# Expert stages of a two-layer hybrid block on one core: instructions kept in the order of the source, and the one-hot matrix of the slot table built three weight units earlier

## The chip, the core and the metric

The kernel runs on one core of a Trainium2 chip. The metric is the device time of one execution in microseconds (us). The core's engines are named as the profile names them: PE (TensorE matmuls; PEld its weight loads), DVE (VectorE), ACT (ScalarE), POOL (GpSimd) and SP (SyncE, which here only issues transfers). Each engine works through its own list of instructions in order, and an instruction that waits holds up all that stand behind it on that engine.

## The reference

Two layers of a block with four mixers, then an expert-choice feed-forward net. The change touches only the last part, which in short is:

```python
def expert_choice_ffn(h, w_router, w_gate, w_up, w_down):
    n, dm = h.shape[1], h.shape[2]
    cap = EC_FACTOR * n // N_EXPERTS
    aff = jax.nn.softmax(jnp.einsum('bnd,de->bne', h, w_router).astype(jnp.float32), axis=-1)
    g, idx = lax.top_k(aff.swapaxes(1, 2), cap)
    xs = jax.vmap(lambda hb, ib: hb[ib])(h, idx)
    act = jax.nn.silu(jnp.einsum('becd,edf->becf', xs, w_gate)) * jnp.einsum('becd,edf->becf', xs, w_up)
    ys = jnp.einsum('becf,efd->becd', act, w_down) * g[..., None].astype(h.dtype)
    ...
```

There are 16 experts, a model width of 1024 and an expert width of 512. Each expert takes 128 of the 1024 tokens; in layer 0 it also takes 32 of the 256 context tokens with the same weights. Layer 1 needs no context.

## The kernel before

Mixers and expert stage of a layer are Python generators which a planner interleaves; when the expert stage runs, it is alone. What the generators emit is not yet the order on the chip: the framework's scheduler puts the instructions of every engine in an order of its own, from its own costs, unless a stretch is traced under `manual_schedule`, where the order of the source stays.

The expert stage is the function `experts`. Its weights come in 12 units of 512 KB for each expert: four units `k` = 0 to 3 (gate, up, gate, up), four of down, and `k` = 4 to 7. A round, the body of `for e in range(17)`, does for expert `e`: `gate_up` for `k` = 0 to 3; after `k` = 1 `turn(e - 1)`, which transposes the activations of the expert before; after `k` = 3 `prep(e + 2)`; in layer 0 `ctx`, the context's matmuls on the raw weights of the four units; `down(e - 1)`; `parts`, which transposes the gathered tokens of expert `e + 1`; `gate_up` for `k` = 4 to 7; `ctx` again; and `activate`.

`prep` makes the slot table: `onehot` compares each token's place with the slot number in eight DVE instructions (TENSOR_SCALAR, tile `M<-rc,pos`), eight small PE matmuls (`ps<-M,M`, 128x5) turn them into token numbers and gates, and POOL gathers the 128 tokens (`W<-dr,it`).

A weight unit passes four stations. SP loads it into one of 10 raw buffers (tile `C`). `issue` then splits it: ACT writes the high part (`A<-C`), DVE or, for two units of a round, POOL the low part (`A<-C,A`). The PE uses both. `gate_up` and `down` each call `issue` once, for the unit that stands 5 (layer 0) or 8 (layer 1) places further on. A raw buffer is free again in layer 0 when the context's matmuls on it are done, and in layer 1 when it is split; only then can SP load the unit that is 10 places further on:

```python
ahead, ring, raws = (5, 7, 10) if need else (8, 10, 10)
```

Of the kernel before, what the change touches and what calls it, by code (L numbers as in the profile page):

```python
# [163 lines left out]
class Model:  # L164
# [1573 lines left out]
                                    op0=ALU.is_equal)  # L1738
        return O

    def slots(self, e):

        nc = self.nc
        O = self.onehot(0, e, 8)
        po = self.p()
        for j in range(8):
            nc.tensor.matmul(po[:, 0:5], O[:, j], self.R[0][:, j, e, :], start=j == 0, stop=j == 7)
        sc = self.t("s1", [128, 5])
        nc.vector.tensor_copy(sc, po[:, 0:5])
        it = self.t("it", [128, 1], U32, bufs=4)  # L1750
        vt = self.t("vt", [128, 1], bufs=4)
        nc.vector.scalar_tensor_tensor(it, sc[:, 1:2], 128.0, sc[:, 0:1], op0=ALU.mult, op1=ALU.add)
        nc.vector.tensor_reduce(vt, sc[:, 2:5], axis=AX.X, op=ALU.add)
        return it, vt
# [32 lines left out]
    def experts(self, l, need, base, basec, h2d, h2c):  # L1787
# [5 lines left out]
        ahead, ring, raws = (5, 7, 10) if need else (8, 10, 10)  # L1793
# [30 lines left out]
        def issue(early=False):  # L1824
            nonlocal unit
            if not raw:
                return
            w = raw.pop(0)
            u = unit % ring
            hi, lo = rows[u], rows[ring + u]  # L1830
            nc.scalar.activation(hi, w, AF.Copy)
            (nc.gpsimd if early or unit % 6 == 5 else nc.vector).tensor_sub(lo, w, hi.bitcast(F32))
            unit += 1
            ready.append((w, hi, lo))
            if not need:
                fetch(1)

        def prep(e):
            it, vt = self.slots(e)
            X[e] = (self.gather(h2d, it), it, vt)  # L1840

        def gather_ctx(g):
# [15 lines left out]
        def parts(x):  # L1858

            x = x.rearrange("p (u n k) -> p u k n", u=4, k=2)  # L1860
            xh = self.t("W", [128, 8, 128], F32R)
            xl = self.t("W", [128, 8, 128], F32R)
            for hf in range(2):
                pt = self.p([128, 4, 128])
                for i in range(4):
                    nc.tensor.transpose(pt[:, i, :], x[:, 2 * hf + i // 2, i % 2], self.ident)
                hs = slice(4 * hf, 4 * hf + 4)
                nc.scalar.activation(xh[:, hs], pt, AF.Copy)
                nc.vector.tensor_sub(xl[:, hs], pt, xh[:, hs].bitcast(F32))
            return xh, xl  # L1870

        def gate_up(e, u, g, p):

            xh, xl = XT[e]
            w, hi, lo = ready.pop(0)
            for k in range(2):
                c = slice(512 * k, 512 * k + 512)
                for pas, (xx, ww) in enumerate(((xh, hi), (xl, hi), (xh, lo))):
                    nc.tensor.matmul(p, xx[:, 2 * u + k], ww[:, c], start=(u == 0 and k == 0 and pas == 0),
                                     stop=(u == 3 and k == 1 and pas == 2))  # L1880
            issue()
            return u, g, w

        def ctx(e, units, pc):

            cs = slice(32 * (e % 4), 32 * (e % 4) + 32)
            for u, g, w in units:
                for k in range(2):
                    for q in range(4):
                        nc.tensor.matmul(pc[32 * q:32 * q + 32, 128 * g:128 * g + 128], XC[e // 4][:, 2 * u + k, cs],  # L1890
                                         w[:, 512 * k + 128 * q:512 * k + 128 * q + 128], start=(u == 0 and k == 0 and g == 0),
                                         stop=(u == 3 and k == 1 and g == 1))
                fetch(1)
# [12 lines left out]
        def turn(e):  # L1906

            act, actc = ACT.pop(e)
            pt = self.p([128, 4, 128])
            for i in range(4):  # L1910
                nc.tensor.transpose(pt[:, i, :], act[:, 128 * i:128 * i + 128], self.ident)
            ah = self.t("M", [128, 4, 128], F32R)
            al = self.t("M", [128, 4, 128], F32R)
            nc.scalar.activation(ah, pt, AF.Copy)
            nc.vector.tensor_sub(al, pt, ah.bitcast(F32))
            ct = None
            if need:
                pt = self.p([128, 4, 128])
                nc.tensor.transpose(pt[:, 0, :], actc, self.ident)
                ct = self.t("M", [128, 128])  # L1920
                nc.scalar.activation(ct, pt[:, 0, :], AF.Copy)
            AT[e] = (ah, al, ct)

        def down(e):
            _, it, vt = X.pop(e)
            ah, al, ct = AT.pop(e)
            py = [self.p() for _ in range(2)]
            units = []
            for f in range(4):
                w, hi, lo = ready.pop(0)  # L1930
                for pas, (xx, ww) in enumerate(((ah, hi), (al, hi), (ah, lo))):
                    for hf in range(2):
                        nc.tensor.matmul(py[hf], xx[:, f], ww[:, 512 * hf:512 * hf + 512],
                                         start=(f == 0 and pas == 0), stop=(f == 3 and pas == 2))
                issue()
                units.append(w)
                yield "s"
            if need:
                pyc = self.p()
                for f, w in enumerate(units):  # L1940
                    for q in range(4):
                        nc.tensor.matmul(pyc[32 * q:32 * q + 32, :256], ct[:, 32 * f:32 * f + 32],
                                         w[:, 256 * q:256 * q + 256], start=f == 0, stop=f == 3)
                    fetch(1)
            ys = self.t("W", [128, D])
            for hf in range(2):
                c = slice(512 * hf, 512 * hf + 512)
                nc.vector.scalar_tensor_tensor(ys[:, c], py[hf], vt, G5[hf], op0=ALU.mult, op1=ALU.mult)
            nc.gpsimd.indirect_dma_start(out=base, out_offset=bass.IndirectOffsetOnAxis(ap=it, axis=0),
                                         in_=ys, in_offset=None, compute_op=ALU.add)  # L1950
            if need:
                yc = self.t("M", [128, 256])
                nc.vector.scalar_tensor_tensor(yc, pyc[:, :256], self.vc[:, e:e + 1], G5c, op0=ALU.mult, op1=ALU.mult)
                nc.gpsimd.indirect_dma_start(out=basec.rearrange("n (q d) -> (n q) d", q=4),
                                             out_offset=bass.IndirectOffsetOnAxis(ap=self.ic4[:, e:e + 1], axis=0),
                                             in_=yc, in_offset=None, compute_op=ALU.add)
# [17 lines left out]
            yield 3.0  # L1974
            turn_ctx(0)
        yield from self.wait(f"route{l}.0")
        prep(0)
        yield True
        prep(1)
        issue()  # L1980
        yield 3.0
        XT[0] = parts(X[0][0])
        while len(ready) < ahead:
            issue()
        for e in range(17):
            if e < 16:
                pg, pu = self.p(), self.p()
                pc = self.p() if need else None
                units = []
                for k in range(4):  # L1990
                    units.append(gate_up(e, k // 2, k % 2, (pg, pu)[k % 2]))
                    if k == 1 and e:
                        turn(e - 1)
                    if k == 3 and e + 2 < 16:
                        prep(e + 2)
                    yield "s"
                if need:
                    ctx(e, units, pc)
                    yield "s"
            else:  # L2000
                turn(e - 1)
            if e:
                yield from down(e - 1)
                yield "s"
            if e < 16:
                if e + 1 < 16:
                    if need and (e + 1) % 4 == 0:
                        turn_ctx((e + 1) // 4)
                    XT[e + 1] = parts(X[e + 1][0])
                    if need and e % 4 == 1 and e < 12:  # L2010
                        gather_ctx(e // 4 + 1)
                units = []
                for k in range(4, 8):
                    units.append(gate_up(e, k // 2, k % 2, (pg, pu)[k % 2]))
                    yield "s"
                if need:
                    ctx(e, units, pc)
                activate(e, pg, pu, pc)
            yield "s"

    def layer(self, l):
        need = l == 0
# [82 lines left out]
```

## Time and profile before

| what | value |
|---|---|
| median of 3 runs | 2949.53 us (2943.96 to 2954.22) |
| the profiled execution, and its span | 2941.95 us, 2940.1 us |
| PE busy over the span | 2499.6 us, 85% |
| DVE busy over the span | 1930.1 us, 66% |
| ACT, POOL busy | 1186.9 us (40%), 916.7 us (31%) |
| mean granted TensorE clock | 0.906 |

The expert stages are a small part of the program's instructions, but two stretches of the span: about 1130 to 1655 us (layer 0) and about 2580 to 2940 us (layer 1). A granted clock of 1.00 is 2.4 GHz and one of 0.50 is 1.2 GHz; a mean between them is a share of time at each. Nearly all instructions are recorded in the line of one helper (L160), so the rows are told apart by their tiles. The time outside the span in the profiled execution is 1.85 us.

### The profile page before, as it was taken

How to read it: one execution, taken by the hardware profiler on the slowest of the kernel's cores; microseconds unless marked ns; L12 is line 12 of the kernel's file. 1: busy time of each engine (PE TensorE's matmuls, PEld its weight loads, DVE VectorE, ACT ScalarE, POOL GpSimd, SP SyncE). 2: the span in 40 equal slices, each digit the busy share in tenths (PEclk: the TensorE clock that was granted, in tenths of full speed). 3: DMA queues.
4: the chain of work that ended last, by engine and by line, in shares of the span. 5: the costliest groups of instructions: out<-in, count | busy, mean ns of one | idle time of the engine just before them, and what ended most of it. 6: DMA issues, size and time to landing. Idle time of an engine off the chain costs nothing. (4 is left out here: it accounts for less than half of the span.)

```text
span 2940.1 us, 50544 instructions
## 1 busy us (share of the span) xinstructions
PE 2499.6 (85%) x19427; PEld 1879.6 (64%) x19427; DVE 1930.1 (66%) x3894; ACT 1186.9 (40%) x2010; POOL 916.7 (31%) x930
## 2 busy tenths in 40 slices
PE   6879989989997875888889699879878988579997
PEld 3658877545554654666656488779655556467776
DVE  5444575567775546666666656681778765679996
ACT  3354223244352122444445444342353342356664
POOL 3212332234421131233233432421353411324443
PEclk8889999999998887988889799989979999789998
DMA  6222235485214343666667711132331024569996
GB/s 241 61 65 63 75 107 162 154 276 200 65 63 142 111 168 116 226 237 224 229 205 263 229 47 37 51 97 77 115 111 53 22 93 138 213 225 338 347 342 207
DMA packets 243440, 455.45 MB, mean 155 GB/s; under 512 B 25688, under 2 KB 155096, under 8 KB 242176
## 3 DMA queue, kind: packets, MB, share of 16 engines
q1 hardware_dynamic: 190176, 365.75, 36.2%
q0 software_dynamic: 12096, 37.75, 5.7%
q10 hardware_dynamic: 40928, 48.72, 4.7%
q8 instruction: 153, 2.51, 0.4%
q14 instruction: 87, 0.71, 0.1%
HBM read 377.55 MB, written 74.60 MB: 154 GB/s over the span
## 5 line engine op out<-in xcount | busy, mean ns | idle before, releaser
L160 PE MATMUL ps<-A,W 128*128 128x512 f32 (+3 forms) x4160 | 968.9, 378 | 67.8 <-ACT W L160 31.5
L160 PEld LDWEIGHTS ps<-A,W 128*128 128x128 f32 x4160 | 735.9, 194 | 221.1 <-ACT W L160 35.4
L160 DVE TENSOR_TENSOR A<-C,A 128x1024 fp32r<-128x1024 f32 x310 | 458.0, 1496 | 155.3 <-ACT A L160 149.7
L160 ACT ACTIVATE A<-C 128x1024 fp32r<-128x1024 f32 x384 | 399.6, 1058 | 325.5 <-DMA C<-in_moe_w_gate_dram 119.7
L160 ACT ACTIVATE M<-ps 128x512 f32<-128x512 f32 (+6 forms) x576 | 264.2, 468 | 486.9 <-PE ps L160 404.5
L160 POOL TENSOR_TENSOR A<-C,A 128x1024 fp32r<-128x1024 f32 x74 | 200.9, 2719 | 214.0 <-ACT A L160 213.7
L160 PE MATMUL ps<-A,M 128*128 128x512 f32 x768 | 204.7, 420 | 1.1 <-ACT M L160 0.7
L160 PE MATMUL ps<-W,A 128*128 128x256 f32 x1344 | 191.7, 299 | 9.8 <-DVE A L160 8.8
L160 PEld LDWEIGHTS ps<-W,A 128*128 128x128 f32 x1344 | 176.5, 202 | 12.3 <-DVE A L160 9.3
L160 PE MATMUL ps<-C,A 128*32 128x128 f32 (+1 forms) x2528 | 183.0, 331 | 0.0
L160 PEld LDWEIGHTS ps<-A,M 128*128 128x128 f32 x768 | 151.8, 202 | 36.6 <-issue 5.2
L160 PE MATMUL ps<-M,M 128*128 128x64 f32 (+3 forms) x968 | 126.0, 254 | 54.6 <-DVE M L160 44.0
L160 POOL TENSOR_TENSOR C<-C,M 128x512 f32<-128x512 f32 x76 | 111.8, 1483 | 193.0 <-ACT M L160 132.8
L160 PE MATMUL ps<-cf,M 128*128 128x128 f32 (+3 forms) x416 | 75.3, 304 | 101.1 <-DVE M L160 67.9
L160 DVE TENSOR_TENSOR C<-C,M 128x512 f32<-128x512 f32 (+2 forms) x196 | 129.4, 672 | 40.7 <-ACT M L160 39.3
L160 PEld LDWEIGHTS ps<-C,A 128*32 128x32 f32 (+1 forms) x2528 | 143.6, 140 | 9.4 <-issue 5.3
L160 PE MATMUL ps<-A 96*128 96x512 f32 (+3 forms) x368 | 132.7, 417 | 9.4 <-ACT A L160 4.0
L160 PEld LDWEIGHTS ps<-cf,M 128*128 128x128 f32 (+2 forms) x416 | 54.6, 153 | 131.9 <-DVE M L160 51.9
L160 PE MATMUL ps<-A,C 128*128 128x512 f32 x352 | 135.2, 415 | 1.6 <-DVE C L160 1.4
L160 ACT ACTIVATE W<-ps 128x512 fp32r<-128x512 f32 (+2 forms) x156 | 66.1, 476 | 162.9 <-PE ps L160 162.2
L160 POOL TENSOR_TENSOR W<-W,C 128x512 f32<-128x512 f32 x33 | 49.6, 1520 | 259.4 <-DVE W L160 154.8
L160 ACT ACTIVATE C<-ps 128x512 f32<-128x512 f32 (+4 forms) x116 | 53.8, 469 | 180.3 <-PE ps L160 166.1
(239 smaller groups left out, 3949.7 us busy)
## 6 DMA issues: line engine op xcount, KB each, us to landing
C<-in_moe_w_gate_dram SPq DMA_DIRECT2D x128, 512.0 KB, 5.0
C<-in_moe_w_up_dram SPq DMA_DIRECT2D x128, 512.0 KB, 5.3
C<-in_moe_w_down_dram SPq DMA_DIRECT2D x128, 512.0 KB, 6.8
W<-in_ada_w_dram SPq DMA_DIRECT2D x80, 512.0 KB, 4.5
W<-in_w_in_dram SPq DMA_DIRECT2D x40, 512.0 KB, 3.7
C<-dr SPq DMA_DIRECT2D x29, 512.0 KB, 4.1
dr<-M ACTq DMA_DIRECT2D x114, 128.0 KB, 2.4
M<-dr SPq DMA_DIRECT2D x46, 256.0 KB, 5.1
```

Source lines behind the costliest of these rows:

```text
L160: return f(*args, **kw)
```

## The change

It puts the rounds of the expert stage under `manual_schedule`, and it calls `onehot` for expert `e + 2` after `k` = 0 instead of inside `prep` after `k` = 3; `prep` gets the finished matrix. Apart from the deeper indentation the core of the diff is this.

```diff
-    def slots(self, e):
+    def slots(self, e, O=None):
...
-        O = self.onehot(0, e, 8)
+        O = self.onehot(0, e, 8) if O is None else O
...
-        def prep(e):
-            it, vt = self.slots(e)
+        def prep(e, O=None):
+            it, vt = self.slots(e, O)
...
+        with self.tc.manual_schedule():
...
+                        if k == 0 and e + 2 < 16:
+                            O = self.onehot(0, e + 2, 8)
                         if k == 3 and e + 2 < 16:
-                            prep(e + 2)
+                            prep(e + 2, O)
```

Outside the expert stages the lists of the engines stay as they were, but for a weight split in layer 0 that moves across the routing and two rows at the start of layer 1.

On PE, in a round of layer 0, this stood behind the last matmuls of unit `k` = 3 (`ps_15888`) before. `W_15788` and `W_15789` are the high and low parts of the tokens, `A` the split weights, `ps_15887` the gate sums, `M_15938` the one-hot matrix, `ps_15889` the context's sums.

```order
L160 MATMUL ps_15888<-A_14850,W_15788 128x512
L160 MATMUL ps_15888<-A_14850,W_15789 128x512
L160 MATMUL ps_15888<-A_14851,W_15788 128x512
L160 MATMUL ps_15887<-A_14851,W_15788 128x512
L160 MATMUL ps_15887<-A_14851,W_15789 128x512
L160 MATMUL ps_15887<-A_14852,W_15788 128x512
L160 LDWEIGHTS M_15938
L160 MATMUL ps_15947<-M_14829,M_15938 128x5
L160 MATMUL ps_15889<-C_15704,A_14853 32x128
```

The same place now (`M_15900` is the one-hot matrix, `ps_15891` the context's sums, and the eight small matmuls stand in a row):

```order
L160 MATMUL ps_15890<-A_14850,W_15790 128x512
L160 MATMUL ps_15890<-A_14850,W_15791 128x512
L160 MATMUL ps_15890<-A_14851,W_15790 128x512
L160 LDWEIGHTS M_15900
L160 MATMUL ps_15949<-M_14829,M_15900 128x5
...
L160 MATMUL ps_15891<-C_15706,A_14853 32x128 x8
```

The three matmuls on `ps_15887` are the first half of unit `k` = 4, which the scheduler had drawn ahead of the slot table, the context and `down`; they now stand behind `parts` with the other half.

On DVE, in a round of layer 0, from the products of `activate` (`M_17049`, and `M_17052` for the context) to the slot table's copy out of PSUM, before:

```order
L160 TENSOR_TENSOR M_17049<-M_17049,ps_16768 128x512
L160 TENSOR_TENSOR A_14851<-C_16941,A_14850 128x1024
L160 TENSOR_TENSOR A_14851<-C_16947,A_14850 128x1024
L160 TENSOR_TENSOR M_17052<-M_17052,ps_16769 128x128
L160 TENSOR_TENSOR A_14851<-C_17017,A_14850 128x1024
L160 TENSOR_TENSOR A_14852<-C_17027,A_14850 128x1024
L160 TENSOR_TENSOR M_17082<-ps_17076,M_17081 128x512
L160 TENSOR_TENSOR A_14852<-C_17037,A_14850 128x1024
L160 TENSOR_SCALAR M_17107<-rc_647,pos_1896_15026 128x128 x8
L160 COPY s_2170_17125<-ps_17116 128x5
```

and now:

```order
L160 TENSOR_TENSOR M_17051<-M_17051,ps_16770 128x512
L160 TENSOR_TENSOR M_17054<-M_17054,ps_16771 128x128
L160 TENSOR_TENSOR A_14851<-C_17019,A_14850 128x1024
L160 TENSOR_SCALAR M_17069<-rc_647,pos_1896_15026 128x128 x8
L160 TENSOR_TENSOR A_14852<-C_17029,A_14850 128x1024
L160 TENSOR_TENSOR M_17093<-ps_17087,M_17092 128x512
L160 TENSOR_TENSOR A_14852<-C_17039,A_14850 128x1024
L160 COPY s_2170_17127<-ps_17118 128x5
```

The eight TENSOR_SCALAR moved from behind the third weight split of the round to behind the first, and the product for `activate` moved behind the splits of `k` = 4 to 7.

On DVE, in a round of layer 1, before and now (the splits `A<-C,A` ahead of the product are not shown):

```order
L160 TENSOR_TENSOR M_31759<-M_31759,ps_31568 128x512
L160 TENSOR_TENSOR A_30982<-C_31608,A_30980 128x1024
L160 TENSOR_TENSOR A_30982<-C_31658,A_30980 128x1024
L160 TENSOR_TENSOR A_30982<-C_31669,A_30980 128x1024
L160 TENSOR_TENSOR M_31792<-ps_31786,M_31791 128x512
L160 TENSOR_SCALAR M_31817<-rc_647,pos_3995_31148 128x128 x8
```

```order
L160 TENSOR_TENSOR M_31764<-M_31764,ps_31573 128x512
L160 TENSOR_TENSOR A_30985<-C_31622,A_30983 128x1024
L160 TENSOR_SCALAR M_31780<-rc_647,pos_3995_31151 128x128 x8
L160 TENSOR_TENSOR M_31806<-ps_31800,M_31805 128x512
```

The low part of the turned activations (`M_31792`, now `M_31806`) and the one-hot matrix now stand behind one split instead of three; one more split than before stands ahead of the product.

## Rows read from the trace of the kernel before

**Rows 1.** Busy time of each engine by stretch: length, engines, granted clock, DMA share, GB/s.

```profile
1155.27:1594.73 439.46, 377.50 (x3317) 272.88 (x3313) 293.98 (x379) 196.99 (x243) 139.05 (x67) 0.89 0.68 224
1594.73:1619.47 24.74, 24.40 (x250) 19.05 (x246) 19.11 (x18) 15.06 (x19) 10.72 (x5) 1.00 0.86 288
2607.26:2886.21 278.95, 254.70 (x1197) 200.42 (x1196) 254.16 (x348) 182.11 (x205) 115.94 (x52) 0.97 0.98 335
2886.21:2904.04 17.83, 17.83 (x84) 14.93 (x85) 17.80 (x16) 13.67 (x16) 7.90 (x3) 1.00 0.99 332
```

**Rows 2.** Groups of PE, 1155.27 to 1594.73: busy us, mean ns | idle before.

```profile
L160 PE MATMUL ps<-A,W 128*128 128x512 f32 x624 | 161.8, 405 | 30.6 <-ACT A L160 20.9 <-DVE A L160 9.7
...
L160 PE MATMUL ps<-M,M 128*128 128x5 bf16 x104 | 13.2, 180 | 21.9 <-DVE M L160 21.9
L160 PE MATMUL ps<-cf,M 128*128 128x128 f32 x65 | 11.5, 282 | 8.8 <-DVE M L160 8.8
L160 PE MATMUL ps<-cf,A 128*128 128x128 f32 x24 | 3.7, 296 | 0.0
```

**Rows 3.** PE in order of time, one round of layer 0 [idle before <-releaser].

```profile
1333.44 0.73 PE L160 MATMUL ps<-A,W 128*128 128x512 f32 x2 [0.93 <-ACT A L160]
...
1337.33 0.18 PE L160 MATMUL ps<-M,M 128*128 128x5 bf16 x1 [1.83 <-DVE M L160]
...
1340.32 2.36 PE L160 MATMUL ps<-C,A 128*32 128x128 f32 x38
```

**Rows 4.** PE in order of time, round 14 of layer 0, which has no slot table.

```profile
1597.59 0.60 PE L160 MATMUL ps<-cf,M 128*128 128x128 f32 x4
...
1601.54 1.95 PE L160 MATMUL ps<-C,A 128*32 128x128 f32 x64
```

**Rows 5.** All engines in order of time, the round of rows 3.

```profile
1334.87 3.54 DVE L160 TENSOR_SCALAR M<-rc,pos 128x128 bf16<-128x128 bf16 x8
...
1341.87 0.33 SPq L1820 DMA_DIRECT2D C<-in_moe_w_gate_dram  x1
...
1349.28 1.06 ACT L160 ACTIVATE A<-C 128x1024 fp32r<-128x1024 f32 x1 [1.01 <-DMA C<-in_moe_w_gate_dram]
```

**Rows 6.** All engines in order of time, round 14 of layer 0.

```profile
1603.16 0.37 SPq L1820 DMA_DIRECT2D C<-in_moe_w_gate_dram  x1
...
1608.60 1.06 ACT L160 ACTIVATE A<-C 128x1024 fp32r<-128x1024 f32 x1 [0.20 <-DMA C<-in_moe_w_gate_dram]
```

**Rows 7.** DVE groups, layer 0, 1155.27 to 1594.73.

```profile
L160 DVE TENSOR_TENSOR A<-C,A 128x1024 fp32r<-128x1024 f32 x131 | 195.4, 1497 | 118.0 <-ACT A L160 117.6
...
L160 DVE SCALAR_TENSOR_TENSOR W<-ps,vt,M 128x512 f32<-128x512 f32 x26 | 19.4, 745 | 0.0
L160 DVE TENSOR_TENSOR W<-ps,W 128x512 fp32r<-128x512 f32 x26 | 16.6, 682 | 0.0
L160 DVE TENSOR_TENSOR M<-M,ps 128x512 f32<-128x512 f32 x14 | 9.6, 686 | 3.4 <-ACT M L160 1.9 <-issue 1.3
...
L160 DVE SCALAR_TENSOR_TENSOR M<-ps,vc,M 128x256 f32<-128x256 f32 x13 | 6.2, 479 | 0.0
```

**Rows 8.** PE in order of time at the start of layer 0's rounds.

```profile
1138.88 0.42 PE L160 MATMUL ps<-M,M 128*128 128x5 bf16 x8
```

**Rows 9.** All engines in order of time, one round of layer 1.

```profile
2721.04 1.38 DVE L160 TENSOR_SCALAR M<-rc,pos 128x128 bf16<-128x128 bf16 x8
2721.33 0.34 PE L160 MATMUL ps<-M,M 128*128 128x5 bf16 x2 [2.38 <-DVE M L160]
```

**Rows 10.** Who waited for whom: ACT, layer 0, 1155.27 to 1594.73.

```profile
ACT A L160 <- DMA C<-in_moe_w_gate_dram: 114.4, 30, 8.9
```

**Rows 11.** Busy time by stretch, as rows 1: ten microseconds of layer 1.

```profile
2700.00:2710.00 10.00, 10.00 (x53) 8.03 (x54) 8.88 (x16) 6.32 (x8) 4.19 (x2) 1.00 1.00 380
```

**Rows 12.** Groups of PE, 2607.26 to 2886.21.

```profile
L160 PE MATMUL ps<-M,M 128*128 128x5 bf16 x104 | 14.8, 177 | 17.1 <-DVE M L160 17.1
```

More of the change, by code (lines that the diff above doesn't have):

```diff
@@ L1976, in experts @@
         yield from self.wait(f"route{l}.0")
[L1977 to L1983, printed above, removed]
-            issue()
[L1985 to L1994, printed above, removed]
-                        prep(e + 2)
-                    yield "s"
[L1997 to L2003, printed above, removed]
-                yield "s"
[L2005 to L2019, printed above, removed]
@@ new lines, in experts @@
+        with self.tc.manual_schedule():
+            prep(0)
+            yield True
+            prep(1)
+            issue()
+            yield 3.0
+            XT[0] = parts(X[0][0])
+            while len(ready) < ahead:
+                issue()
+            for e in range(17):
+                if e < 16:
+                    pg, pu = self.p(), self.p()
+                    pc = self.p() if need else None
+                    units = []
+                    for k in range(4):
+                        units.append(gate_up(e, k // 2, k % 2, (pg, pu)[k % 2]))
+                        if k == 1 and e:
+                            turn(e - 1)
+                        if k == 0 and e + 2 < 16:
+                            O = self.onehot(0, e + 2, 8)
+                        if k == 3 and e + 2 < 16:
+                            prep(e + 2, O)
+                        yield "s"
+                    if need:
+                        ctx(e, units, pc)
+                        yield "s"
+                else:
+                    turn(e - 1)
+                if e:
+                    yield from down(e - 1)
+                    yield "s"
+                if e < 16:
+                    if e + 1 < 16:
+                        if need and (e + 1) % 4 == 0:
+                            turn_ctx((e + 1) // 4)
+                        XT[e + 1] = parts(X[e + 1][0])
+                        if need and e % 4 == 1 and e < 12:
+                            gather_ctx(e // 4 + 1)
+                    units = []
+                    for k in range(4, 8):
+                        units.append(gate_up(e, k // 2, k % 2, (pg, pu)[k % 2]))
+                        yield "s"
+                    if need:
+                        ctx(e, units, pc)
+                    activate(e, pg, pu, pc)
+                yield "s"
```

## The prediction, made before the changed kernel ran

> **What bounds the kernel now.** I first read busy time by stretch [rows 1]. The reader should see that the two expert stages are limited by different things. Thirteen rounds of layer 0 (expert 1 to 13) take 439.46 us, 33.80 a round. PE is busy 377.50 of that at a granted clock of 0.89, DVE 293.98, and the DMA engines have a share of 0.68. No engine is full, so PE loses time to waits and to the clock. Thirteen rounds of layer 1 take 278.95 us, 21.46 a round; there PE (254.70) and DVE (254.16) are nearly as full as each other, 19.59 and 19.55 a round, and the DMA share is 0.98, 21.03 a round. Layer 1 has little to give.
>
> Next the groups of PE in layer 0, for the idle time ahead of each [rows 2]. Of 439.46 − 377.50 = 61.96 us idle, 30.6 stand ahead of the `gate_up` matmuls, 21.9 ahead of the eight slot matmuls and 8.8 ahead of the transposes of `turn`. Then PE in order of time through one round, to see which `gate_up` matmuls wait [rows 3]: not a random one, but the three of unit 4 that stand ahead of the slot table (0.93 us on ACT's split and, behind it, on DVE's). They use a unit that has only just been split, while context and `down`, whose operands are ready, stand behind them. After them the first slot matmul waits 1.83 us for the one-hot matrix.
>
> The waits cost twice. After them the clock is at its lower level: 38 context matmuls take 2.36 us, 62 ns each, where 64 take 1.95 us, 30 ns each, in round 14 [rows 3, 4]. Round 14 is the same round without slot table and gather, with the same weight units but not the three matmuls' stall: 24.74 us, PE busy 24.40, clock 1.00 [rows 1].
>
> **The change, part by part, layer 0.** Behind unit 3 PE now finds eight slot matmuls, context and `down`; unit 4's matmuls wait until `parts` is done, by when their splits are long over. The matrix is made after unit 0. Its eight DVE instructions cost 3.54 us in the round read [rows 5], 1.38 in a round of layer 1 [rows 9], and PE reaches the slot matmuls only after three more units (12 matmuls take 3.0 us, two units) and `turn`. So they should cost 0.42 us, as where the matrix was ready [rows 8]. The cost on DVE is not new, only earlier: it delays the splits of units four places further on, and ahead of these PE has the rest of the four units, slots, context (1.95 us [rows 4]) and `down`. I take 0 for that; if that cover were gone, the whole 3.54 a round would show.
>
> The new round is therefore round 14 plus what it lacks: 24.74 [rows 1] + 0.42 [rows 8] + 0.28 for the context tokens' transposes (3.7 / 13 [rows 2]) = 25.44 us. The gather costs PE nothing, it is DMA. For the transposes of `turn` I add some waiting: they waited 8.8 / 13 = 0.68 us a round [rows 2], and their product on DVE now stands behind the splits of units 4 to 7; round 14's 24.74 holds 0.34 idle already, so 0.26 more, about the rest. That gives 25.7 us and 13 × (33.80 − 25.7) = **105.3 us**. As a check by parts: the idle 61.96 goes but for some 8 (0.34 + 0.26 a round), and PE's busy time falls from 377.50 / 13 = 29.04 to 24.40 + 0.42 + 0.28 = 25.10 a round, 51 us; 54 + 51 = 105. About half of the gain is thus the clock's.
>
> The bounds for this term: from below 25.44 (108.7 us gained). From above the loop in which the next stall would sit. Weights are requested when the context's matmuls free raw buffers; the third such unit must land, is split, and DVE does four splits, the two `ys`, `yc`, the two `xl` and the product ahead of `turn`. From landing that is 1.06 for ACT's split [rows 5] + 4 × 1.497 + 2 × 0.745 + 0.479 + 2 × 0.682 + 0.686 = 10.01 on DVE [rows 7], then from `turn` to the next context 1601.54 − 1597.59 = 3.95 [rows 4] and 0.42 for the slots: 15.44. The time from the start of slots and context until that unit landed was 1349.28 − 1337.33 = 11.95 us in the round read [rows 3, 5] and 1608.60 − 1601.54 = 7.06 in round 14 [rows 4, 6]. So the loop gives between 22.5 and 27.4 us, and binds above 25.44 − 15.44 = 10.0. I place the landing at 9.0: at full clock the request comes 1603.16 − 1601.54 = 1.62 after the context's start, and from request to split took 1349.28 − 1341.87 = 7.41 in the round with a gather [rows 4 to 6]. Then the loop is 24.5 and does not bind, with a margin of 0.9. The upper end 27.4 (83 us gained) stays for the range.
>
> DMA is not the limit in layer 0: 0.68 × 33.80 = 23.0 us a round, a share of 0.89 at 25.7; round 14 ran at 0.86 [rows 1].
>
> **Layer 1.** The same edit removes PE's wait for the matrix: 17.1 us ahead of the slot matmuls [rows 12], 2.38 in the round shown [rows 9], of 278.95 − 254.70 = 24.25 idle. What is next late: a round cannot be shorter than DVE's 19.55 or PE's 19.59, and by the DMA engines' busy time not than 21.03 [rows 1]. So the gain lies between 13 × 0.43 = 5.6 and 13 × 1.87 = 24.3. The engines can move more than they do: ten microseconds went at 380 GB/s [rows 11], against 335, at which a round's 335 × 21.46 = 7.19 MB would take 18.9. I take 20.85, close to the DMA end, since with a share of 0.98 hardly a gap is left to fill, a little under it because that share includes transfers that queue behind each other: 13 × 0.61 = **8 us**. Below the bound I allow 0, if a freed buffer only moves the wait to the next unit.
>
> The Trainium skill, on the page "DMA: Bandwidth & Descriptors", in its opening table of specifications, gives about 358 GB/s as the limit of HBM for one core. By it an estimate of layer 1's round is 7.19 MB / 358 = 20.1 us, the gain there at most 17.7 and the whole result some 10 us faster than mine, not the 24.3 that 380 GB/s would leave to DVE and PE; the trace's 380 over ten microseconds stands against its figure as a hard limit, the mean of 335 does not.
>
> **Elsewhere 0.** Rounds 14 to 16 have no slot table, round 0 had it ready [rows 8], mixers keep their order. The split that moves across the routing is one of 1.06 us on ACT [rows 5], worth nothing or that.
>
> **Sum.** 105.3 + 8 = 113.3 us off the profiled execution's 2941.95 is 2828.7. That execution lies 2949.53 − 2941.95 = 7.6 under the median of the runs; carried over, 2836.
>
> **Rivals.**
> *The loop binds* (landing above 10.0). For it: the round read with a gather shows 11.95, and a shorter round raises the DMA share. Against: part of the 11.95 is the half clock. At 27.4 a round: 83 + 0 to 8, so 2858 to 2866. Chance 0.15.
> *The clock stays low.* Only the idle goes, 33.80 − 61.96 / 13 = 29.03 a round: 62 + 0 to 8 us, 2879 to 2887. For it: PE still has single short waits and small matmuls each round. Against: round 14, clock 1.00. Chance 0.07.
> *Layer 1 goes down to its DVE and PE.* 105 + 24, 2820. For it: 380 GB/s in places. Against: the share of 0.98. Chance 0.08.
> *The change does nothing:* the ten raw buffers and the landing set layer 0's pace already, and a removed wait comes back at the next unit. For it: ACT waits 114.4 us for gate weights alone [rows 10]. Against: round 14 has the same units and buffers. Within 0.3%, that is 8.8 us, about what a measurement of this kernel can tell from no change. Chance 0.04.
> *Slower.* The fixed order puts `turn`'s product, which the scheduler had let pass, behind splits that wait for weights, so PE stands at `turn` until they land. Its loop is landing + 15.44, longer than the 33.80 of now above 18.36 us of landing; with layer 1's 8 us against it, 0.3% slower from 18.36 + 16.8 / 13 = 19.65. At 21 us: 36.4 a round, 34 lost less 8, 2976. Against: 7.06 and 11.95. Chance 0.04.
> *My forecast* has the rest, 0.62, with 25.44 to 26.3 a round of layer 0 (98 to 109) and 20.1 to 21.4 of layer 1 (1 to 18): 2823 to 2851.
>
> **How the numbers follow.** The range 2816 to 2870 takes in the forecast, the loop and layer 1's lower bound (0.85) and leaves out the low clock and the two without gain. Faster by over 0.3%: 0.62 + 0.15 + 0.07 + 0.08 = 0.92; within 0.3% 0.04; slower 0.04.
>
> **What the profile after would show.** Right: layer 0's rounds near 25.7 us at a clock of 1.00 and a DMA share near 0.9; no idle ahead of unit 4's matmuls; slot matmuls eight in a row, 0.42 us, with no wait in either layer; PE's remaining idle ahead of `turn`'s transposes, under 0.7 a round; layer 1's rounds near 20.9 us with DMA at 0.99. Wrong: waits of 2 us on `turn`'s product (the loop); a clock near 0.9 without idle; ACT's waits for weights in layer 0 grown as PE's fell; DVE with splits late behind the one-hot instructions.

## The result, and the profile after

The changed kernel takes 2843.21 us (median of 4, 2841.87 to 2850.83) against 2946.74 us (median of 4) for the kernel before: ratio 0.9654, 95% interval 0.9623 to 0.9686. The forecast of 2836 is 7 us off, inside its range. Its parts are less well met. By stretches of the two profiled executions (2941.95 and 2842.43 us), of the 99.5 us that went, 439.46 − 355.05 = 84.4 lie in thirteen rounds of layer 0 (105.3 forecast), 278.95 − 273.45 = 5.5 in thirteen of layer 1 (8 forecast) and 9.6 elsewhere (0 forecast). The span outside these two stretches was 2221.7 us before and 2212.1 after. In the profiles of the eleven other kernels below it was 2213 to 2225 where layer 1 has the fixed order and 2226 to 2231 where it has not, so a few microseconds of the 9.6 may belong to the fixed order and the rest is the spread of executions; which part was not settled. That the total came so close is in part luck: layer 0 gave 20.9 us less than forecast and layer 1 2.5 less, the 9.6 from elsewhere made up for some of it, and the 7.6 by which the median before lay over the profiled execution, which the forecast added, is only 0.8 in the changed kernel.

Busy time of the changed kernel by stretch answers to [rows 1]: rounds 1 to 13 and round 14 of layer 0, then rounds 1 to 13 of layer 1.

```profile
1154.29:1509.34 355.05, 338.11 (x3318) 263.07 (x3314) 279.30 (x378) 199.60 (x244) 131.27 (x69) 0.98 0.84 279
1509.34:1535.35 26.01, 24.37 (x250) 18.98 (x246) 20.00 (x20) 15.14 (x19) 8.61 (x5) 1.00 0.81 267
2514.97:2788.42 273.45, 249.61 (x1198) 201.78 (x1197) 263.51 (x352) 179.13 (x209) 120.74 (x53) 0.96 1.00 352
```

The reader sees 27.31 us a round in layer 0, not 25.7, with the clock at 0.98, and PE idle for 16.94 us (355.05 − 338.11) where it was 61.96. Round 14, which the change has no work in, is 1.3 us longer than before: something besides the slot table was touched. Layer 1 has 21.03 us a round.

The groups of PE in rounds 1 to 13 of layer 0 answer to [rows 2]: busy us, mean ns, idle before and its releaser.

```profile
L160 PE MATMUL ps<-A,W 128*128 128x512 f32 x625 | 154.3, 399 | 0.0
...
L160 PE MATMUL ps<-M,M 128*128 128x5 bf16 x104 | 13.1, 175 | 6.1 <-DVE M L160 6.0
L160 PE MATMUL ps<-cf,M 128*128 128x128 f32 x65 | 9.9, 284 | 9.8 <-DVE M L160 9.8
```

The wait of the `gate_up` matmuls is gone, as forecast. The slot matmuls kept 6.1 of 21.9 us, which was not forecast, and the transposes of `turn` wait 9.8 instead of 8.8. The busy time of the slot matmuls has hardly fallen either (13.1 us after 13.2): as the rows below show, they follow DVE's eight instructions, 1.32 us beside 1.39, where 4.6 us are enough for all 13 rounds once the matrix is ready (matrix ahead, below). One round in order of time, all engines, shows both waits.

```profile
1425.13 2.98 POOL L160 TENSOR_TENSOR A<-C,A 128x1024 fp32r<-128x1024 f32 x1
1425.32 5.02 DVE L160 TENSOR_TENSOR A<-C,A 128x1024 fp32r<-128x1024 f32 x2 [1.09 <-ACT A L160]
...
1430.26 0.87 DVE L160 TENSOR_TENSOR M<-M,ps 128x512 f32<-128x512 f32 x2
...
1430.99 0.77 PE L160 MATMUL ps<-cf,M 128*128 128x128 f32 x5 [1.78 <-DVE M L160]
...
1432.77 1.06 ACT L160 ACTIVATE A<-C 128x1024 fp32r<-128x1024 f32 x1 [5.60 <-DMA C<-in_moe_w_down_dram]
1433.86 1.23 DVE L160 TENSOR_TENSOR A<-C,A 128x1024 fp32r<-128x1024 f32 x1 [2.72 <-ACT A L160]
...
1435.00 1.39 DVE L160 TENSOR_SCALAR M<-rc,pos 128x128 bf16<-128x128 bf16 x8
...
1435.31 1.32 PE L160 MATMUL ps<-M,M 128*128 128x5 bf16 x8 [0.81 <-DVE M L160]
...
1436.56 3.05 PE L160 MATMUL ps<-C,A 128*32 128x128 f32 x64
```

The product for `turn` (1430.26) stands behind two splits that take 5.02 us, while POOL makes one; two such splits take 2 × 1.22 where POOL makes none (an experiment below). The matrix (1435.00) stands behind the split of `k` = 0, which waits for ACT, and ACT for a down weight to land. Behind the second wait the granted clock is 0.61 over the context's 64 matmuls, and they take 3.05 us instead of 1.95 [rows 4].

A correction to the section on the kernel: in layer 0 the unit that `issue` splits stands six places on, not five, because `prep(1)` is followed by one more `issue` before the rounds begin. So the splits at `k` = 6 and 7 are those for the first two units of `down`. One sum of the prediction hangs on this. Its loop counts four splits on DVE, from that of the third unit which the context's matmuls free to the product for `turn`. With six places there are five, in each of the 13 rounds of the changed kernel's trace. At the prediction's own 1.497 us for a split its loop is 25.9 us instead of 24.5, above the 25.44 that it was compared with.

In layer 1 the wait of the slot matmuls is gone and PE waits at `turn` instead, 23.8 us. The groups of PE, 2514.97 to 2788.42 (before [rows 12]):

```profile
L160 PE MATMUL ps<-cf,M 128*128 128x128 f32 x53 | 10.0, 316 | 23.8 <-DVE M L160 23.8
L160 PE MATMUL ps<-M,M 128*128 128x5 bf16 x104 | 7.1, 170 | 0.0
```

### The profile page after: what moved, and what is told of

Read it like the earlier page. It is cut to its first block, busy times and chain, and to the rows that moved or that the text cites. A ratio compares the mean times of both kernels' runs of the same rounds, so it can differ in the third digit from the quotient of the medians.

```text
span 2840.6 us, 50547 instructions
## 1 busy us (share of the span) xinstructions
PE 2446.1 (86%) x19427; PEld 1865.0 (66%) x19427; DVE 1910.6 (67%) x3894; ACT 1181.4 (42%) x2010; POOL 910.9 (32%) x930
## 5 line engine op out<-in xcount | busy, mean ns | idle before, releaser
L160 DVE TENSOR_TENSOR A<-C,A 128x1024 fp32r<-128x1024 f32 x310 | 443.7, 1459 | 93.7 <-ACT A L160 87.4
L160 ACT ACTIVATE A<-C 128x1024 fp32r<-128x1024 f32 x384 | 392.0, 1058 | 187.9 <-DMA C<-in_moe_w_down_dram 64.5
L160 POOL TENSOR_TENSOR A<-C,A 128x1024 fp32r<-128x1024 f32 x74 | 208.0, 2815 | 214.6 <-ACT A L160 161.1
L160 PE MATMUL ps<-A,M 128*128 128x512 f32 x768 | 186.7, 399 | 0.9 <-ACT M L160 0.9
L160 PEld LDWEIGHTS ps<-A,M 128*128 128x128 f32 x768 | 142.8, 190 | 36.1 <-issue 3.1
L160 PE MATMUL ps<-C,A 128*32 128x128 f32 (+1 forms) x2528 | 148.0, 290 | 0.0
L160 PEld LDWEIGHTS ps<-C,A 128*32 128x32 f32 (+1 forms) x2528 | 134.8, 127 | 6.9 <-issue 4.6
L160 PE MATMUL ps<-M,M 128*128 128x64 f32 (+3 forms) x968 | 116.8, 251 | 23.1 <-DVE M L160 12.6
```

What stands on the lines that cost most here:

```text
L160: return f(*args, **kw)
```

## The experiments

First a table of all kernels: the time as measured, its ratio to the kernel before with its 95% interval, and the mean length of rounds 1 to 13 in the profiled execution. The kernel before was timed again beside every group of kernels (medians of 2946.74 to 2954.63 us), so ratios compare better than times.

| kernel | us, median | ratio | layer 0 | layer 1 |
|---|---|---|---|---|
| before | 2946.74 | 1 | 33.80 | 21.46 |
| the change | 2843.21 | 0.9654 (0.9623 to 0.9686) | 27.31 | 21.03 |
| early matrix alone | 2816.13 | 0.9543 (0.9525 to 0.9561) | 25.40 | 19.88 |
| fixed order alone | 2959.35 | 1.0032 (1.0018 to 1.0046) | 33.98 | 21.63 |
| matrix after unit 2, no fixed order | 2947.99 (one run) | not timed | 34.11 | 21.29 |
| change, product ahead | 2848.01 | 0.9655 (0.9639 to 0.9671) | 26.90 | 21.19 |
| change, matrix ahead | 2838.54 | 0.9636 (0.9611 to 0.9662) | 26.15 | 21.24 |
| change, both ahead | 2827.58 | 0.9583 (0.9564 to 0.9602) | 25.53 | 21.40 |
| change, all splits on DVE | 2815.90 | 0.9532 (0.9516 to 0.9548) | 27.07 | 18.95 |
| both ahead, all splits on DVE | 2800.59 | 0.9477 (0.9460 to 0.9494) | 25.38 | 19.02 |
| early matrix alone, all splits on DVE | 2806.49 | 0.9510 (0.9489 to 0.9531) | 24.94 | 20.03 |
| the same, POOL one split a round in layer 1 | 2806.03 | 0.9494 (0.9476 to 0.9513) | 24.90 | 19.56 |
| early matrix, all splits on DVE, fixed order in layer 1 alone | 2791.64 | 0.9476 (0.9458 to 0.9494) | 24.87 | 18.99 |

**The two parts of the change apart.** First the early matrix without the fixed order, here against the kernel before:

```diff
+                    if k == 0 and e + 2 < 16:
+                        O = self.onehot(0, e + 2, 8)
                     if k == 3 and e + 2 < 16:
-                        prep(e + 2)
+                        prep(e + 2, O)
```

> The matrix is built after unit 0, the rest stays with the scheduler. In its lists PE no longer runs unit 4 ahead of the slot table, so the early matrix has taken that away as well, and DVE has the product for turn between the weight splits and the matrix ahead of all splits of the round. My theory (PE lost time to the premature matmuls and to the matrix, and what is left after the change sits behind DVE's splits): layer 0 at 25.5 to 27 us a round, layer 1 near 21, 2825 to 2845 us, as fast as the whole change or faster. Rival (the fixed order is what gains, the early matrix alone only saves the slot wait of 1.7 us a round): layer 0 near 31 us, 2900 to 2920 us.

Then the fixed order, with the matrix in `prep` as before, against the changed kernel:

```diff
-                        if k == 0 and e + 2 < 16:
-                            O = self.onehot(0, e + 2, 8)
                         if k == 3 and e + 2 < 16:
-                            prep(e + 2, O)
+                            prep(e + 2)
```

> Fixed order, but the matrix is built in prep after unit 3, behind two splits more. My theory: unit 4's matmuls no longer wait, the slot matmuls do (2 to 5 us a round, behind splits that wait for weights), and the clock drops after that wait: layer 0 at 29 to 32 us a round, 2880 to 2915 us. Rival (the order alone is what gains): under 28 us a round, 2840 to 2855 us.

The early matrix alone takes 2816.13 us, 9 less than the range of my theory and 27 less than the whole change; layer 1, near 21 by that theory, came to 19.88. The fixed order alone is a little slower than the kernel before, so that both its expectations were missed, mine by 44 us. The early matrix is the whole gain, and the fixed order gives some of it back. Busy time by stretch of the early matrix alone (layer 0, layer 1, and five rounds of layer 1):

```profile
1162.44:1492.58 330.14, 324.15 (x3315) 252.82 (x3314) 275.04 (x378) 196.66 (x242) 142.62 (x67) 1.00 0.89 299
2509.22:2767.67 258.45, 245.92 (x1197) 197.25 (x1197) 250.52 (x342) 182.48 (x205) 127.50 (x52) 0.99 1.00 360
2548.84:2643.22 94.38, 92.03 (x461) 74.55 (x460) 94.23 (x136) 72.90 (x81) 51.05 (x21) 1.00 1.03 386
```

Layer 0's round is 25.40 us at clock 1.00: the 25.44 that the prediction built up from round 14. Of the fixed order alone, the groups of PE in layer 0, 1160.24 to 1602.01:

```profile
L160 PE MATMUL ps<-A,W 128*128 128x512 f32 x624 | 152.4, 396 | 0.0
...
L160 PE MATMUL ps<-M,M 128*128 128x5 bf16 x104 | 17.3, 187 | 73.3 <-DVE M L160 73.3
```

The 30.6 us in front of unit 4's matmuls [rows 2] are gone here too, and nothing is won: the slot matmuls wait 73.3 instead of 21.9. The wait only moved. Why the early matrix needs no fixed order can be read in its lists. PE, the place that the section on the change shows (`M_15898` is the matrix):

```
L160 MATMUL ps_15888<-A_14850,W_15788 128x512
L160 MATMUL ps_15888<-A_14850,W_15789 128x512
L160 MATMUL ps_15888<-A_14851,W_15788 128x512
L160 LDWEIGHTS M_15898
L160 MATMUL ps_15947<-M_14829,M_15898 128x5
```

DVE, from the products to the low part of the turned activations:

```
L160 TENSOR_TENSOR M_17049<-M_17049,ps_16768 128x512
L160 TENSOR_TENSOR A_14851<-C_16947,A_14850 128x1024
L160 TENSOR_TENSOR M_17052<-M_17052,ps_16769 128x128
L160 TENSOR_SCALAR M_17067<-rc_647,pos_1896_15026 128x128 x8
L160 TENSOR_TENSOR A_14851<-C_17017,A_14850 128x1024
L160 TENSOR_TENSOR A_14852<-C_17027,A_14850 128x1024
L160 TENSOR_TENSOR M_17091<-ps_17085,M_17090 128x512
```

The scheduler, with the matrix early, no longer draws unit 4 ahead of the slot table. And it leaves the product between two splits and sets the matrix ahead of the split of `k` = 0, one split earlier than the fixed order has it.

**How early is early.** The same with `k == 2` in the place of `k == 0`:

> Scheduler's order, the matrix asked for after unit 2 instead of after unit 0. On DVE it then stands where it stood before the change, behind the third split and the low part of the turned activations. If what gains is DVE's place for the matrix: nothing is won, layer 0 at 32 to 34.5 us a round, 2925 to 2955 us. Rival (any earlier call is enough): under 28 us a round, under 2860 us.

One run without an interval, 2947.99, and 34.11 us a round in layer 0: as before the change. In its list the matrix stands on DVE behind the low part of the turned activations and a split, just where it was, and PE waits for unit 4 ahead of the slot table again (33.4 us in 13 rounds). What counts is the place in DVE's list, not the place of the call.

That old place has a second drawback, which the prediction did not see. In the round of rows 5, POOL begins a split of its own just ahead of the matrix:

```profile
1334.58 2.65 POOL L160 TENSOR_TENSOR A<-C,A 128x1024 fp32r<-128x1024 f32 x1 [7.62 <-ACT A L160]
```

POOL's split ends at 1337.23, and the first slot matmul starts at 1337.33 [rows 3]. Of the matrix's eight instructions the first takes 2.40 us and each other one 0.24. It is so in all 13 rounds of layer 0: the matrix takes 3.48 to 3.54 us beside a split of POOL's, and 1.38 or 1.39 in the changed kernel, where none falls on it. So about 2.1 us of each late matrix are POOL's. The fixed order alone has them as well, and PE waits 73.3 / 13 = 5.6 us a round there, so they are not all of it. How much of the gain comes from the earlier place as such, and how much from getting away from POOL's split, stays open: the kernel before with all splits on DVE was not run.

**What the fixed order gives back.** Two rows of DVE moved within it, one at a time. The product for `turn` ahead of the splits at `k` = 6 and 7:

```diff
-            issue()
+            if not hold:
+                issue()
...
-                        units.append(gate_up(e, k // 2, k % 2, (pg, pu)[k % 2]))
+                        units.append(gate_up(e, k // 2, k % 2, (pg, pu)[k % 2], k > 5))
...
                     activate(e, pg, pu, pc)
+                    issue()
+                    issue()
```

> The changed kernel with the splits for units 6 and 7 issued behind activate, so that DVE makes the product for turn ahead of them. If turn's remaining waits (9.8 us over 13 rounds of layer 0, 23.8 in layer 1) come from the product's place behind splits: they go, with the clock's drop after them, layer 0 at 26.2 to 26.8 us a round, 2826 to 2836 us. Rival (weights land too late, so the wait moves to the slot table or to unit 0): 27.3 us a round as now, 2838 to 2848 us.

The matrix ahead of the split at `k` = 0:

```diff
+                        if k == 0 and e + 2 < 16:
+                            O = self.onehot(0, e + 2, 8)
                         units.append(gate_up(e, k // 2, k % 2, (pg, pu)[k % 2]))
...
-                        if k == 0 and e + 2 < 16:
-                            O = self.onehot(0, e + 2, 8)
```

> The changed kernel with the matrix built ahead of unit 0's split instead of behind it. If the remaining slot waits (6.0 us over 13 rounds of layer 0) come from that one split waiting for its weight: they go, with the clock's drop after them, layer 0 at 26.4 to 26.9 us a round, 2830 to 2838 us. Rival (the loop is set by the landing of weights, whatever DVE's order): 27.3 us a round as now, 2838 to 2848 us.

And both together:

> Fixed order as in the changed kernel, with both rows moved: the product for turn ahead of the splits for units 6 and 7, the matrix ahead of unit 0's split. My theory now (the fixed order loses against the early matrix alone only by these two places on DVE, and each alone passes its wait on to the other): no wait of turn or of the slot table over 0.5 us, layer 0 at 25.3 to 26 us a round, layer 1 at 19 to 20.3, 2808 to 2826 us. Rival (other rows of the fixed order, on ACT or PE, cost as well): layer 0 above 26.2 or layer 1 above 20.8, 2830 us or more.

The groups of PE in layer 0 with the product ahead, 1162.15 to 1511.89:

```profile
L160 PE MATMUL ps<-C,A 128*32 128x128 f32 x1664 | 55.0, 288 | 0.0
...
L160 PE MATMUL ps<-M,M 128*128 128x5 bf16 x104 | 16.8, 179 | 9.0 <-DVE M L160 8.9
...
L160 PE MATMUL ps<-cf,M 128*128 128x128 f32 x66 | 9.5, 272 | 0.0
```

With the matrix ahead, 1162.67 to 1502.61:

```profile
L160 PE MATMUL ps<-C,A 128*32 128x128 f32 x1664 | 50.8, 274 | 0.0
...
L160 PE MATMUL ps<-cf,M 128*128 128x128 f32 x66 | 10.1, 282 | 12.4 <-DVE M L160 12.4
L160 PE MATMUL ps<-M,M 128*128 128x5 bf16 x104 | 4.6, 167 | 0.0
```

Each row takes away its own wait and passes part of it to the other: product ahead, `turn` 0 but the slots 9.0; matrix ahead, slots 0 but `turn` 12.4. With the product alone the rival was right in the main: the wait moves, layer 0 is 0.4 us a round shorter (26.90) and the whole is no faster (2848.01). With the matrix alone layer 0 is a little better than expected (26.15) and the time just outside (2838.54); its interval overlaps that of the change. Both together bring layer 0 to 25.53, as expected, so in layer 0 these two places are what the fixed order costs. In layer 1 the expectation failed: 21.40 us a round, the rival's side, though `turn` waits no more, and the time, 2827.58, lies between the two. There PE waits for the low part of the turned activations (12.7 us ahead of `down`) and for the slots (4.2), and the clock is 0.96.

**Whether the overlap of the two engines' splits is the cause in layer 1.** The weight splits of POOL go to DVE:

```diff
-            (nc.gpsimd if early or unit % 6 == 5 else nc.vector).tensor_sub(lo, w, hi.bitcast(F32))
+            (nc.gpsimd if early else nc.vector).tensor_sub(lo, w, hi.bitcast(F32))
```

In the early matrix alone:

> The early matrix alone, scheduler's order, and the two weight splits a round that POOL makes given to DVE. Layer 1's rounds without an overlap of the two engines' splits ran at 18.87 us with DVE full (94.23 of 94.38 us); a split beside POOL's takes DVE up to 3.4 us instead of 1.22. If DVE's own work is the bound of layer 1: two more splits of 1.13 each, 21.1 us a round, layer 0 unchanged at 25.4, 2828 to 2838 us. Rival (the overlap with POOL costs more than the two splits): layer 1 at or below 19.9, 2800 to 2816 us.

In the changed kernel:

> The changed kernel with POOL's two splits a round given to DVE. If turn's waits in layer 0 (product behind splits that take up to 4.7 us beside POOL's) come from the overlap: layer 0 at 25.5 to 26.5 us a round, layer 1 at 20.5 to 21.3, 2815 to 2835 us. Rival (they come from weights that land late, in front of the product whatever a split takes): layer 0 at 27.3 or more with DVE longer, 2843 to 2860 us.

In the one with both rows ahead:

> Fixed order with product and matrix moved ahead, and all splits on DVE. If place and overlap are separate causes, both gains add: layer 0 at 24.6 to 25 us a round, layer 1 at 19.5 to 20.5, 2798 to 2812 us, as with the scheduler's order. Rival (the fixed order costs in layer 1 for another reason, such as the low part of the turned activations behind a split): layer 1 at 20.8 to 21.5, 2815 to 2828 us.

DVE's groups in layer 1, first the changed kernel (2514.97 to 2788.42):

```profile
L160 DVE TENSOR_TENSOR A<-C,A 128x1024 fp32r<-128x1024 f32 x131 | 186.7, 1473 | 0.9 <-issue 0.4
L160 DVE TENSOR_SCALAR M<-rc,pos 128x128 bf16<-128x128 bf16 x104 | 28.8, 347 | 0.0
```

then the same with all splits on DVE (2513.11 to 2759.41):

```profile
L160 DVE TENSOR_TENSOR A<-C,A 128x1024 fp32r<-128x1024 f32 x157 | 183.6, 1218 | 0.3 <-issue 0.2
L160 DVE TENSOR_SCALAR M<-rc,pos 128x128 bf16<-128x128 bf16 x104 | 18.0, 249 | 0.0
```

157 splits cost DVE less than 131 did (183.6 against 186.7 us), and the matrix 18.0 instead of 28.8. What POOL took off DVE, DVE lost again by waiting for POOL. With all splits on DVE the changed kernel goes from 2843.21 to 2815.90, and nearly all of it is in layer 1 (18.95 instead of 21.03). The time is inside my range by luck: layer 0 stays at 27.07, where I expected 25.5 to 26.5, and layer 1 is shorter than the 20.5 that I expected at best. PE's groups in layer 0 (1159.98 to 1511.88):

```profile
L160 PE MATMUL ps<-M,M 128*128 128x5 bf16 x104 | 15.9, 178 | 9.5 <-DVE M L160 9.5
L160 PE MATMUL ps<-cf,M 128*128 128x128 f32 x66 | 9.6, 273 | 1.3 <-DVE M L160 1.2
```

The wait of `turn` fell there (9.8 to 1.3 us) and that of the slots rose (6.1 to 9.5). So the overlap was the cause of most of the one; the other stays as long as the matrix stands behind the late weight. With both rows ahead and all splits on DVE the two gains add, 2800.59, as expected, with layer 0 a little longer than that (25.38) and layer 1 shorter (19.02).

My expectation for the early matrix alone with all splits on DVE (slower, layer 1 at 21.1) was wrong as well: 20.03, close to the rival's 19.9, and 2806.49, inside its range, since I priced two more splits and not what the others save. But it is no gain in layer 1 either (19.88 with POOL's splits). Layer 0 is 0.5 us a round shorter, and the intervals of the two kernels overlap.

**One split a round left with POOL in layer 1**, `unit % 12 == 5` there and none in layer 0:

> The early matrix alone, scheduler's order; POOL keeps one split a round in layer 1 and none in layer 0. DVE full at 11 splits in layer 1: 18.85 + 1.13, 19.9 us a round less what overlaps no longer cost; layer 0 at 24.8 as with all splits on DVE. If the overlaps of DVE and POOL set layer 1's extra over 18.85: 19.0 to 19.7 a round, 2790 to 2804 us. Rival (DVE is simply full at 20 us either way): 2803 to 2812 us.

Layer 1 has 19.56 us a round instead of 20.03, within the expected 19.0 to 19.7, but the time, 2806.03, is that of the kernel with none, as the rival had it: nothing that can be measured.

**The best of both.** All splits on DVE, the early matrix, and the fixed order in layer 1 alone:

```diff
-        with self.tc.manual_schedule():
+        with nullcontext() if need else self.tc.manual_schedule():
```

> The early matrix in both layers, all splits on DVE, the fixed order in layer 1 alone; layer 0 stays with the scheduler. If the layers' rounds are independent of each other: layer 0 at 24.7 to 25.0 us a round, layer 1 at 18.9 to 19.1, 2789 to 2801 us. Rival (fixed order in both with product and matrix ahead was as good in layer 0): 2799 to 2806 us.

Its busy time by stretch (layer 0, layer 1):

```profile
1160.27:1483.64 323.37, 321.63 (x3314) 253.31 (x3313) 262.66 (x405) 196.43 (x240) 77.99 (x41) 1.00 0.91 305
2487.59:2734.43 246.84, 241.77 (x1197) 192.75 (x1196) 246.19 (x378) 179.93 (x209) 38.05 (x26) 1.00 1.03 384
```

2791.64 us, 0.9476 (0.9458 to 0.9494). PE is busy 321.63 of 323.37 us in layer 0. Against both rows ahead in a fixed order (0.9477) the ratios do not separate it, though layer 0's rounds are 0.5 us shorter.

## Why the prediction was right, and where it was not

**Bounds of the kernel, right.** PE lost its time in layer 0 to waits and to the clock, and both went together: clock 0.89 to 0.98, and 1.00 in the early matrix alone.

**The 25.44 us a round, right as an estimate and wrong as a floor**: 25.40 was measured with the early matrix alone, but 24.87 at best.

**Whose gain it is, wrong.** The prediction credited the fixed order with taking unit 4's matmuls out of the way. It does, but alone that moves the wait to the slot table (73.3 us) and wins nothing; the early matrix brings PE's list into that order by itself. The prediction did not ask what each half would do alone.

**The term for layer 0 mis-sized, 84.4 instead of 105.3.** A round is 1.6 us longer than forecast: 0.7 of that is idle time of PE (16.94 / 13 = 1.30, 0.60 forecast) and 0.9 its busy time (338.11 / 13 = 26.01, 25.10 forecast). Two steps failed.

The first is "the loop does not bind, with a margin of 0.9". The landing in it was right: from the first slot matmul to the start of DVE's split of the third unit that the context frees, the 13 rounds take 10.1 us in the mean, where the prediction had 9.0 + 1.06. But from there to the end of the product for `turn` they take 12.6 us, and the prediction had 10.01: there are five splits and not four, and some of them wait for weights or stand beside POOL's. With 3.95 and 0.42 the loop is 27.0 us, about as long as the round. So the rival "the loop binds" was right about the loop; that its 27.4 nearly is the measured 27.31 is chance, for it rests on a landing of 11.95 us. `turn` waits 0.75 us a round, behind splits as that rival had it, but for the overlap with POOL more than for the landing.

The second is that the slot matmuls "should cost 0.42 us, as where the matrix was ready". The matrix stands behind one split that waits for a down weight, so that they wait 0.47 us a round and take 1.01 (13.1 / 13), and the context loses some of its clock behind them (53.8 us, where 50.8 are enough with the matrix ahead). The prediction asked whom the early matrix delays, and not whom it waits for.

**Layer 1: 21.03 measured, between my 20.85 and the 21.46 of before, for another reason than given.** The prediction took 21.03 from the DMA engines' busy time as nearly a floor. It is none: with the same transfers 18.95 to 19.88 us a round were reached, at a DMA share of 1.00 to 1.03. What held the changed kernel there was DVE, busy 263.51 of 273.45 us, its waits for POOL among them. PE felt it ahead of `turn` (23.8 us); yet with the product ahead of the splits the round is no shorter (21.19 and 21.40 us), and with POOL's splits gone it is. The case that I gave 0.08, layer 1 down to DVE and PE (19.55, 19.59), came true in other kernels, and 18.95 shows that these two were no floors either.

**The limit of 358 GB/s.** The best kernel moved 384 GB/s over 246.84 us of layer 1. The page "DMA: Bandwidth & Descriptors" of the Trainium skill, section "Specifications", has about 358 GB/s as the limit of HBM for one core; on this one core the measurement decides against the figure as a limit. The page "HBM Reference" of the Trainium skill, section "Specifications (TRN2)", adds that a core streaming alone measures well above that share, and with that the trace agrees.

**Slower, no change, low clock**: none of the three came. The slower rival's mechanism, `turn`'s product behind late splits, is there, at 0.75 us a round.

**What stays open.** How much of the early matrix's gain is its escape from POOL's split; why `turn`'s waits hardly lower the clock and the slots' do; and why with both rows ahead layer 1 is not faster until POOL's splits go, in more detail than the overlap.

## What to carry to other kernels

When a change has two halves, price each alone: the one that looks like the cause (the premature matmuls) was a follower, and fixing the order by hand fixed also the places that the scheduler had chosen better. In a list that is worked off in order, ask of every row that moves whom it now waits behind, above all if that one waits for a transfer. A high DMA share is no floor as long as no wait of the chain ends on a DMA.

## What the runs showed of the hardware

**DVE's subtraction of two tiles in SBUF waits for POOL's.** A split takes DVE 1.22 us where POOL makes none. In the changed kernel's layer 1, a run of four splits with POOL's among them:

```profile
2761.42 6.77 DVE L160 TENSOR_TENSOR A<-C,A 128x1024 fp32r<-128x1024 f32 x4
...
2763.95 3.16 POOL L160 TENSOR_TENSOR A<-C,A 128x1024 fp32r<-128x1024 f32 x1 [1.77 <-ACT A L160]
...
2768.84 1.11 PE L160 MATMUL ps<-cf,M 128*128 128x128 f32 x4 [3.60 <-DVE M L160]
```

Four splits took 6.77 us instead of 4 × 1.22 = 4.9, about 2 us more, the greater part of POOL's 3.16. They end at 2768.19, 1.08 us after POOL's (2767.11). That is the rule in this trace: 35 splits of DVE in the changed kernel take over 1.5 us, and each of them ends 1.08 or 1.09 us after a split of POOL's. The page "SBUF — State Buffer" of the Trainium skill, section "Who interferes with whom", says that a DVE instruction with two inputs in SBUF contends with a GpSimd instruction that reads SBUF, and that what the two share is an exclusive lock. The trace agrees.

**The same wait costs the clock or not.** In the fixed order alone, two rounds of layer 1 have the same wait of 1.43 us ahead of the slot matmuls:

```profile
2661.74 1.31 PE L160 MATMUL ps<-M,M 128*128 128x5 bf16 x8 [1.43 <-DVE M L160]
2662.92 5.72 PE L160 MATMUL ps<-A,M 128*128 128x512 f32 x24
...
2811.17 1.33 PE L160 MATMUL ps<-M,M 128*128 128x5 bf16 x8 [1.43 <-DVE M L160]
2812.35 7.10 PE L160 MATMUL ps<-A,M 128*128 128x512 f32 x24
```

Behind the second the 24 matmuls of `down` take 7.10 us instead of 5.72. The busy time of five such rounds in a row, and of the seven behind them:

```profile
2636.26:2739.69 103.43, 96.28 (x461) 77.40 (x460) 85.79 (x135) 68.83 (x80) 45.82 (x21) 1.00 1.00 353
2739.69:2895.10 155.41, 145.40 (x645) 116.08 (x644) 120.19 (x189) 96.29 (x112) 63.93 (x29) 0.92 0.97 334
```

At clock 1.00 a round is 20.69 us, at 0.92 it is 22.20. So 1.5 us of a round hang on the clock, and the waits in the rows are the same. In layer 0 the wait of `turn` was cheaper still: in the changed kernel with the matrix ahead it is 12.4 us, and the context runs at its full rate (50.8 us for 1664 matmuls, 55.0 with the product ahead and the slots' 9.0).
